# Turning the gated feed-forward tiles with transposing DMAs in two 16-bit planes instead of TensorE transposes

## The chip, the cores and the metric

The kernel runs on one core of a Trainium2 chip. The metric is the device time of one execution in microseconds (us), as the median of several runs. The profile is one execution taken by the hardware profiler. The engines are TensorE (PE for its matmuls, PEld for its weight loads), VectorE (DVE), ScalarE (ACT), GpSimd (POOL) and SyncE (SP). SP and ACT also issue DMAs from their instruction queues; in the tables these issues stand under SPq and ACTq.

## What is computed

A two-layer backbone over 256 latent tokens of width 2048, with 256 context tokens. Layer 0 mixes tokens by neighbourhood attention, layer 1 by a gated spatial MLP; each is followed by a SwiGLU feed-forward block, and every sub-layer is modulated and normalised. The change touches only the feed-forward block, which runs once in each layer, with `D_FF` = 5632:

```python
def swiglu(h, w_in, w_out):
    gate, up = jnp.split(h @ w_in, 2, axis=-1)
    return (jax.nn.silu(gate) * up) @ w_out
...
h = layer_norm(ALPHA * h + g2 * swiglu(modulate(h, sh2, sc2), ffn_w_in[i], ffn_w_out[i]), ln_g[i, 1], ln_b[i, 1])
```

All of it is float32. The kernel keeps that precision by writing each operand as a high and a low part and adding three products.

## The kernel before

**Pieces and splits.** Weights come as pieces of 128 x 1024 float32 (512 KB), loaded by SP into four `raw` buffers (L107, L108). `split_into` (L90) makes the high part with an ACT copy (L91) and the low part with a DVE subtraction (L92). During the feed-forward blocks there are five pairs of buffers for the parts, three of tag A and two of tag B (L116 to L121), so that four pieces are ready ahead of the one in use (`piece`, L125). `mm3` (L85) issues the three matmuls of a product on lines 86, 87 and 88.

**The feed-forward block.** `ffn` (L817) walks over 11 f-blocks of 512 hidden columns. For each it runs `block_T` (L792) twice: first the gate half into two PSUM accumulators `pg` (one for each 128 tokens), then the up half into `pu`. One `block_T` takes eight pieces (k2 = 0 to 7), and each piece feeds 12 matmuls: two token halves, two rows of weights, three products. After the gate half, ACT computes `sg = silu(pg)` (L843); after the up half, DVE multiplies `sg = pu * sg` (L847). That gives the gated tile in two tiles of 128 tokens x 512 columns.

**The turn.** The second projection needs the hidden columns on the partitions. So `flip` (L828) transposes each gated tile: eight TensorE transposes of 128 x 128 against an identity (L833), four into each of two PSUM tiles, and two ACT copies from PSUM to SBUF (L834). `gT` (L825) names the place: 16 hidden blocks in `gTa` and 28 in `gTb`. The two flips of an f-block are handed to the gate half of the next one as `turn`, and `block_T` pops one after its third and one after its fourth piece (L814). Those of the last f-block go into the list `side` (L849).

**The second projection.** `project_out` (L725) takes `gT` slice by slice, splits each into a high and a low part, and multiplies with the 44 pieces of the output weights, in two halves of the columns.

**Work beside it.** `tick` (L206) is called once for each piece. It pops one entry of `side`, and it pays out the modulation dot products: a list of tasks with costs, paid by a credit that grows at a fixed rate per tick (`pace`, L222) and by 0.3 of it (`BUSY`) when the tick also ran a side task. Each dot product is a 512 KB load issued by ACT (L75, into `ad`, six buffers, fetched up to five ahead) and one DVE instruction over 128 x 1024 (L150). In layer 0's feed-forward block this list is `pace(235)` (L872), in layer 1's `pace(160)` (L951).

**Order.** A scheduler orders the instructions of each engine by when they become ready, with program order as the priority. `pin` (L82) keeps an instruction behind everything that was traced before it on its engine. On each engine instructions then run strictly in that order, and an instruction that waits holds up all behind it.

Of the kernel before, what the change touches and what calls it, by code (L numbers as in the profile page):

```python
# [10 lines left out]
F32 = mybir.dt.float32  # L11
F32R = mybir.dt.float32r
BF16 = mybir.dt.bfloat16
AF = mybir.ActivationFunctionType
ALU = mybir.AluOpType
AX = mybir.AxisListType
# [2 lines left out]
P = 128  # L19
D = 2048  # L20
NT = 256
KT = D // P
NB = D // 512
# [20 lines left out]
BUSY = 0.3  # L44
# [8 lines left out]
def hybrid_kernel(ctx: ExitStack, tc: tile.TileContext, i, out):  # L53
    nc = tc.nc
    V, S, T = nc.vector, nc.scalar, nc.tensor
# [6 lines left out]
    ident = outer.tile([P, P], F32, tag="ident", name="ident")  # L62
    eps_t = outer.tile([P, 1], F32, tag="eps", name="eps_t")
    nc.gpsimd.memset(eps_t, EPS)
    warm = outer.tile([P, 1], F32, tag="warm", name="warm")
    tc.keep_in_program_order(S.activation(warm, eps_t, AF.Silu))
    lncol = outer.tile([P, 4, 2, KT], F32, tag="lncol", name="lncol")
# [14 lines left out]
    def pin(ins):  # L82
        return tc.keep_in_program_order(ins)
# [101 lines left out]
    tasks, side = [], []  # L185
    state = {"credit": 0.0, "rate": 0.0}

    def fetch_ahead():
        for t in tasks[:FETCH]:
            if t[3]:  # L190
                t[3]()
                t[3] = None
# [8 lines left out]
    def pop_task():  # L201
        fetch_ahead()
        tasks.pop(0)[2]()
        fetch_ahead()

    def tick(n=1.0):  # L206
        fetch_ahead()
        if side:
            side.pop(0)()
            n *= BUSY  # L210
        state["credit"] += n * state["rate"] if tasks else 0.0
        while tasks and state["credit"] >= tasks[0][1]:
            state["credit"] -= tasks[0][1]
            pop_task()
        if not tasks:
            state["credit"] = 0.0
# [50 lines left out]
    with tc.tile_pool(name="attnX", bufs=1) as px, ExitStack() as late:  # L267
# [21 lines left out]
        with tc.tile_pool(name="st", bufs=1) as st:  # L289
# [9 lines left out]
            held = {}  # L299
# [13 lines left out]
            pin(nc.scalar.dma_start(badj[:, 0], i["ada_b_col"][:, 0]))  # L313
            pin(S.activation(c_pad[:, :, 0:2], c_col, AF.Silu))
            pin(S.activation(c_col, c_col, AF.Silu))
            mod = st.tile([P, 2, KT, 2], F32, tag="mod", name="mod")
# [10 lines left out]
            def dot_dve(kt, t):  # L327
                r = held.pop((kt, t))
                junk = outer.tile([P, D], BF16, tag="ada", name=f"junk{kt}", bufs=ADA)
                for n, (o, bc) in enumerate(((junk, cc_bc), (r, c_bc))):  # L330
# [33 lines left out]
            def modulate(kt):  # L364
                tmp = st.tile([P, 512], F32, tag="tmp", name=f"tmp{kt}", bufs=2)
                for b in range(2):
                    sl = slice(b * 256, (b + 1) * 256)
                    S.activation(
                        tmp[:, sl], xt[kt][:, sl], AF.Identity,
                        bias=mod[:, 1, kt, b : b + 1], scale=mod[:, 0, kt, b : b + 1],  # L370
# [24 lines left out]
            for kt in range(KT):  # L395
# [35 lines left out]
                if kt == 0:  # L431
                    modulate(1)
                    for bc in (c_bc, cc_bc):
                        pin(S.activation(bc, bc, AF.Silu))
                    fetch(2)
# [4 lines left out]
                for at, h, k0 in EARLY:  # L440
                    if at == kt:
                        h += HK0
                        hi, lo = piece()
                        ps = stp_pool.tile([P, 512], F32, tag="a", name=f"eps{h}{k0}")
                        for j in range(EN):
                            c = slice(j * P, (j + 1) * P)
# [29 lines left out]
        def t_tile(name):  # L476
            return mp.tile([P, 512], F32, tag="t", name=name, bufs=2)
# [6 lines left out]
        with tc.tile_pool(name="attnB", bufs=1) as pb:  # L484
# [12 lines left out]
            def proj_q(h):  # L497
# [10 lines left out]
                ql[h] = pb.tile([P, NT], F32R, tag="ql", name=f"ql{h}", bufs=2)  # L508
                S.activation(qh[h], ps[:, 0:NT], AF.Copy, scale=SCALE)
                V.scalar_tensor_tensor(  # L510
# [133 lines left out]
    def affine_tasks(t3, src, name, rs=None):  # L644
        rows = {}

        def run(nb, b):
            def go():
                if b == 0:
                    rows[nb] = [main.tile([P, 512], F32, tag="zt", name=f"lr{name}{nb}{n}", bufs=2) for n in range(2)]  # L650
                    for n in range(2):
                        spread(rows[nb][n], src[n, nb * 512 : (nb + 1) * 512])
                sl = slice(nb * 512, (nb + 1) * 512)
                if rs:
                    normalise(t3, b, nb, rs[b])
                V.tensor_tensor(t3[:, b, sl], t3[:, b, sl], rows[nb][0], ALU.mult)
                V.tensor_tensor(t3[:, b, sl], t3[:, b, sl], rows[nb][1], ALU.add)
            return go

        side.extend(run(nb, b) for nb in range(NB) for b in range(2))  # L660

    class Modulated:
        def __init__(self, ln, layer, tsh, tsc, name):
# [125 lines left out]
                    for b in range(2):  # L789
                        finish(b, st)  # L790

    def block_T(m, ps, held, turn=()):  # L792
        xh, xl = m.xh, m.xl
        turn = list(turn)

        def products(k2, w, b):
            for kk in range(2):
                kt = k2 * 2 + kk
                c, tb = slice(kk * 512, (kk + 1) * 512), slice(b * P, (b + 1) * P)
                mm3(ps[b], xh[:, kt, tb], xl[:, kt, tb], w[0][:, c], w[1][:, c], kt == 0, kt == KT - 1)  # L800

        if held:
            ws = take(HOLD)
            for b in range(2):
                for k2 in range(HOLD):
                    products(k2, ws[k2], b)
            m.rest()
        for k2 in range(HOLD if held else 0, 8):
            with tc.issue_after(m.mark[1]) if held and k2 == HOLD else nullcontext():
                w = piece()  # L810
            for b in range(2):
                products(k2, w, b)
            tick()
            if turn and k2 >= 2:  # L814
                turn.pop(0)()

    def ffn(layer, m, key, name, finish, free, last=False):  # L817
        pg = [acc_tile(f"pg{layer}{b}") for b in range(2)]
        block_T(m, pg, True)
        free.close()  # L820
        with tc.tile_pool(name=f"ffn{layer}", bufs=1) as pf:
            g0 = outer.tile([P, KT, NT], F32, tag="xT", name=f"gTa{layer}")
            g1 = pf.tile([P, FT - KT, NT], F32, tag="gTb", name=f"gTb{layer}")

            def gT(f, n=1):  # L825
                return g0[:, f : f + n, :] if f < KT else g1[:, f - KT : f - KT + n, :]

            def flip(fb, sg, f2):  # L828
                ps = t_tile(f"gt{layer}{fb}{f2}")
                for j in range(2):  # L830
                    c = (f2 * 2 + j) * P
                    for b in range(2):
                        T.transpose(ps[:, j * NT + b * P : j * NT + (b + 1) * P], sg[b][:, c : c + P], ident)  # L833
                S.copy(gT(4 * fb + 2 * f2, 2), ps)  # L834

            turn = []
            for fb in range(FB):
                if fb:
                    pg = [acc_tile(f"pg{layer}{fb}{b}") for b in range(2)]
                    block_T(m, pg, False, turn)  # L840
                sg = [pf.tile([P, 512], F32, tag="sg", name=f"sg{layer}{fb}{b}", bufs=3) for b in range(2)]
                for b in range(2):
                    S.activation(sg[b], pg[b], AF.Silu)  # L843
                pu = [acc_tile(f"pu{layer}{fb}{b}") for b in range(2)]
                block_T(m, pu, False)
                for b in range(2):
                    V.tensor_tensor(sg[b], pu[b], sg[b], ALU.mult)  # L847
                turn = [partial(flip, fb, sg, f2) for f2 in range(2)]
            side[:0] = turn  # L849
            if last:  # L850
                last_rows()

            def extra():
                return outer.tile([P, 4, 1024], F32R, tag="xT", name=f"extra{layer}")

            project_out(FT, lambda f: gT(f)[:, 0, :], key, name, finish, extra, last)


    m = Modulated(0, 0, SH2, SC2, "f0")
# [23 lines left out]

    m = m2[0]
    affine_tasks(h_t, i["ln_row"][1], "a1")
    add_row(1, G1)
    pace(12)
# [9 lines left out]
    for nb in range(NB):  # L897
        ps = [acc_tile(f"gv{nb}{b}") for b in range(2)]
# [8 lines left out]
    def spatial(nb, g2):  # L907
        u = us[nb]
        tp = t_tile(f"uvt{nb}{g2}")
        sp = s_tile(f"sp{nb}{g2}")  # L910
        for j in range(2):
            g = nb * 4 + g2 * 2 + j
            c = slice((g2 * 2 + j) * P, (g2 * 2 + j + 1) * P)
            o = sp[:, j * NT : (j + 1) * NT].rearrange("p (b c) -> p b c", b=2)
            T.matmul(o, ws[:, g, :], vv[:, :, g * P : (g + 1) * P], start=True, stop=True)
            V.scalar_tensor_tensor(u[:, :, c], o, bs[:, g : g + 1], u[:, :, c], ALU.add, ALU.mult)
        for j in range(2):
            c = slice((g2 * 2 + j) * P, (g2 * 2 + j + 1) * P)
            for b in range(2):
                T.transpose(tp[:, j * NT + b * P : j * NT + (b + 1) * P], u[:, b, c], ident)  # L920
        S.copy(uT[:, nb * 4 + g2 * 2 : nb * 4 + g2 * 2 + 2, :], tp)

    for nb in range(NB):
        ps = [acc_tile(f"gu{nb}{b}") for b in range(2)]
# [10 lines left out]
        if nb:  # L935
            for g2 in range(2):
                spatial(nb - 1, g2)
    side.extend((lambda: spatial(NB - 1, 0), lambda: spatial(NB - 1, 1)))
    m3 = []

    def ready_f1():
# [5 lines left out]
    m = m3[0]  # L947
# [126 lines left out]
```

## Time and profile before

| | us |
|---|---|
| median of 3 runs | 2400.12 |
| lowest, highest run | 2399.07, 2402.12 |
| the profiled execution's own time | 2400.89 |
| its span, first to last instruction | 2399.1 |
| DVE busy, share of the span | 1716.8, 72% |
| ACT busy, share of the span | 1121.9, 47% |
| POOL busy, share of the span | 57.4, 2% |
| mean DMA rate | 256 GB/s |

The span is the time from the first to the last instruction; the execution's own time is 1.8 us longer. The first part of the profile gives busy times of each engine. Matmuls are pipelined and their durations overlap, so the mean duration of a matmul is longer than the time from its start to the start of the next one; a stretch's length is therefore read from start times. The second part shows the same in 40 slices of 60 us:

```profile
DVE  4877867677788778788989777686755555556666
ACT  4354434345644444444455554456444444445552
DMA  9977677766689899999989555856767666566563
```

Each digit is a busy share in tenths. The feed-forward block of layer 0 lies in slices 11 to 23, that of layer 1 in slices 28 to 40.

### The profile page before, as it was taken

Reading aid. Unit: us, or ns where it says so; the run is one execution under the profiler, and the core shown is the slowest. Engines: PE = TensorE matmul, PEld = TensorE weight load, DVE = VectorE, ACT = ScalarE, POOL = GpSimd, SP = SyncE. Lnnn points to the kernel's source line nnn. Section 1 sums busy time; section 2 is a strip of 40 time slices with the busy share of each in tenths; the row PEclk is TensorE's granted clock in tenths of the full one; section 3 lists DMA queues with packets and bytes.
Section 4 is the critical chain, followed back from the end, with each engine's and each line's share of the span. In section 5 each row is a group of like instructions: output and inputs, shape, how many; then the busy total and the mean of one; then the engine's idle time right before and its main releaser. Section 6 shows DMA issues by size and latency. Waiting matters only on the chain.

```text
span 2399.1 us, 31422 instructions
## 1 busy us (share of the span) xinstructions
PE 2370.2 (99%) x11628; PEld 1969.3 (82%) x11628; DVE 1716.8 (72%) x2297; ACT 1121.9 (47%) x1546; POOL 57.4 (2%) x63
## 2 busy tenths in 40 slices
PE   8999999999999999999999999999999999999998
PEld 6788888888788888888888788887788888888886
DVE  4877867677788778788989777686755555556666
ACT  4354434345644444444455554456444444445552
POOL 0000000000010000000000021000100000010000
PEclk9999999999999999999999999999999999999999
DMA  9977677766689899999989555856767666566563
GB/s 392 353 259 244 236 249 241 241 221 210 214 298 349 322 333 335 333 334 342 342 292 341 192 192 196 303 187 208 237 231 234 229 233 223 191 197 200 178 209 132
DMA packets 169106, 614.84 MB, mean 256 GB/s; under 512 B 19604, under 2 KB 21972, under 8 KB 164596
## 3 DMA queue, kind: packets, MB, share of 16 engines
q1 hardware_dynamic: 121172, 440.74, 53.6%
q10 hardware_dynamic: 46372, 167.86, 19.8%
q0 software_dynamic: 1408, 4.23, 0.6%
q8 instruction: 91, 1.49, 0.2%
q14 instruction: 63, 0.52, 0.1%
HBM read 610.62 MB, written 2.13 MB: 255 GB/s over the span
## 4 chain that ended last, share of the span: by engine, by line
PE 95%; DVE 2%; ACT 1%; DMA 1%; issue 1%; SPq 0%; POOL 0%; DVEq 0%; ACTq 0%; POOLq 0%
PE pu L87 7%; PE pu L88 7%; PE pu L86 7%; PE pod L86 7%; PE pod L87 6%; PE pod L88 6%; PE pg L88 6%; PE pg L86 6%; PE pg L87 6%; PE vps L86 2%; PE vps L88 2%; PE vps L87 2%; PE kps L87 2%; PE kps L88 2%; PE kps L86 2%; PE qps L86 1%
## 5 line engine op out<-in xcount | busy, mean ns | idle before, releaser
L92 DVE TENSOR_TENSOR lwf<-rwf,hwf 128x1024 fp32r<-128x1024 f32 x320 | 392.1, 1225 | 282.3 <-ACT hwf L91 281.8
L91 ACT CAST hwf<-rwf 128x1024 fp32r<-128x1024 f32 x320 | 336.2, 1051 | 483.7 <-PE pu L88 221.5
L150 DVE SCALAR_TENSOR_TENSOR ad<-ad,c_bc 128x1024 f32<-128x1024 f32 x320 | 388.0, 1219 | 0.0
L86 PE MATMUL pod<-hwd,ghd 128*128 128x512 f32 x684 | 266.5, 390 | 0.0
L87 PE MATMUL pod<-lwd,ghd 128*128 128x512 f32 x684 | 266.3, 389 | 0.0
L88 PE MATMUL pod<-hwd,gld 128*128 128x512 f32 x684 | 265.9, 389 | 0.0
L92 DVE TENSOR_TENSOR lwd<-rwd,hwd 128x1024 fp32r<-128x1024 f32 x172 | 212.1, 1234 | 63.0 <-ACT hwd L91 62.6
L91 ACT CAST hwd<-rwd 128x1024 fp32r<-128x1024 f32 x172 | 180.4, 1049 | 68.5 <-PE pod L88 45.1
L86 PEld LDWEIGHTS pod<-hwd,ghd 128*128 128x128 f32 x684 | 128.4, 188 | 27.0 <-DVE sg L847 0.3
L88 PEld LDWEIGHTS pod<-hwd,gld 128*128 128x128 f32 x684 | 128.4, 188 | 26.7
L87 PEld LDWEIGHTS pod<-lwd,ghd 128*128 128x128 f32 x684 | 128.4, 188 | 26.3
L86 PE MATMUL pg<-hwf,f0h 128*128 128x512 f32 x320 | 126.5, 395 | 0.0
L86 PE MATMUL pg<-hwf,f1h 128*128 128x512 f32 x320 | 126.5, 395 | 0.0
L88 PE MATMUL pg<-hwf,f0l 128*128 128x512 f32 x320 | 124.8, 390 | 0.0
L88 PE MATMUL pg<-hwf,f1l 128*128 128x512 f32 x320 | 124.7, 390 | 0.0
L86 PE MATMUL pu<-hwf,f1h 128*128 128x512 f32 x320 | 124.6, 389 | 0.0
L86 PE MATMUL pu<-hwf,f0h 128*128 128x512 f32 x320 | 124.6, 389 | 0.0
L88 PE MATMUL pu<-hwf,f1l 128*128 128x512 f32 x320 | 124.5, 389 | 0.0
L88 PE MATMUL pu<-hwf,f0l 128*128 128x512 f32 x320 | 124.5, 389 | 0.0
L87 PE MATMUL pu<-lwf,f1h 128*128 128x512 f32 x320 | 124.5, 389 | 0.0
L87 PE MATMUL pg<-lwf,f0h 128*128 128x512 f32 x320 | 124.5, 389 | 0.0
L87 PE MATMUL pu<-lwf,f0h 128*128 128x512 f32 x320 | 124.5, 389 | 0.0
(346 smaller groups left out, 5137.1 us busy)
## 6 DMA issues: line engine op xcount, KB each, us to landing
ad<-in_ada_t ACTq DMA_DIRECT2D x320, 512.0 KB
rwf<-in_w_in_t SPq DMA_DIRECT2D x320, 512.0 KB
rwd<-in_w_out SPq DMA_DIRECT2D x176, 512.0 KB
rwg<-in_w_gin SPq DMA_DIRECT2D x64, 512.0 KB
ap<-in_ada_p SPq DMA_DIRECT2D x20, 1024.0 KB
rwq<-in_w_q SPq DMA_DIRECT2D x32, 512.0 KB
rwo<-in_w_o SPq DMA_DIRECT2D x32, 512.0 KB
rwt<-in_w_in_t SPq DMA_DIRECT2D x32, 512.0 KB
```

What stands on the lines that cost most here:

```text
L86: keep(T.matmul(ps, sh, mh, start=first, stop=False))
L87: keep(T.matmul(ps, sh, ml, start=False, stop=False))
L88: keep(T.matmul(ps, sl, mh, start=False, stop=last))
L91: S.copy(hi, src)
L92: V.tensor_tensor(lo, src, hi.bitcast(F32), ALU.subtract)
L150: pin(V.scalar_tensor_tensor(r, r, 1.0, c_bc[:, half * 1024 : (half + 1) * 1024], ALU.mult, ALU.mult, accum_out=o[:, nt : nt + 1],))
```

## The change

A gated tile is no longer turned by TensorE. Each of its two tiles of 128 x 512 float32 is read as 128 x 512 pairs of 16-bit words. ACT copies the lower words to one plane and the upper words to another (`planes`, two copies). SP issues a transposing DMA for each plane, SBUF to SBUF, 128 x 512 words into four blocks of 128 x 128 (`turn_over`). ACT then copies the turned words of each plane to every second 16-bit place of `gT` (`join`, two copies). The tile tag `planes` has one buffer, `turned` has two, and `sg` goes from three buffers to two.

The six steps of an f-block have fixed places, counted in pieces from the end of its up half: 3, 6, 8, 11, 15 and 20. So `turn` is now a list of lists that runs on through gate halves and up halves, and the last step of an f-block comes in the gate half after the next. `side` holds lists as well, and `tick` multiplies the credit of a tick by `BUSY` once for each task.

```diff
     def tick(n=1.0):
         fetch_ahead()
         if side:
-            side.pop(0)()
-            n *= BUSY
+            for task in side.pop(0):
+                task()
+                n *= BUSY
...
-    def block_T(m, ps, held, turn=()):
+    def block_T(m, ps, held, turn=None):
         xh, xl = m.xh, m.xl
-        turn = list(turn)
...
             tick()
-            if turn and k2 >= 2:
-                turn.pop(0)()
+            if turn:
+                for task in turn.pop(0):
+                    task()
...
-            def flip(fb, sg, f2):
-                ps = t_tile(f"gt{layer}{fb}{f2}")
-                for j in range(2):
-                    c = (f2 * 2 + j) * P
-                    for b in range(2):
-                        T.transpose(ps[:, j * NT + b * P : j * NT + (b + 1) * P], sg[b][:, c : c + P], ident)
-                S.copy(gT(4 * fb + 2 * f2, 2), ps)
+            def flips(fb, sg):
+                wide = [None, None]
+                turned = [None, None]
+
+                def planes(b):
+                    wide[b] = pf.tile([P, 2, 512], U16, tag="planes", name=f"pl{layer}{fb}{b}")
+                    src = sg[b].bitcast(U16).rearrange("p (f w) -> p w f", w=2)
+                    for w in range(2):
+                        S.copy(wide[b][:, w, :], src[:, w, :])
+
+                def turn_over(b):
+                    turned[b] = pf.tile([P, 2, 4, P], U16, tag="turned", name=f"tu{layer}{fb}{b}", bufs=2)
+                    for w in range(2):
+                        pin(nc.sync.dma_start_transpose(turned[b][:, w], wide[b][:, w, :]))
+
+                def join(b):
+                    dst = gT(4 * fb, 4)[:, :, b * P : (b + 1) * P].bitcast(U16)
+                    dst = dst.rearrange("p a (t w) -> p w a t", w=2)
+                    for w in range(2):
+                        S.copy(dst[:, w], turned[b][:, w])
+
+                at = {3: (planes, 0), 6: (turn_over, 0), 8: (planes, 1), 11: (turn_over, 1), 15: (join, 0), 20: (join, 1)}
+                for n, (task, b) in at.items():
+                    while len(turn) <= n:
+                        turn.append([])
+                    turn[n].append(partial(task, b))
...
                     block_T(m, pg, False, turn)
-                sg = [pf.tile([P, 512], F32, tag="sg", name=f"sg{layer}{fb}{b}", bufs=3) for b in range(2)]
+                    block_T(m, pg, False, turn)
+                sg = [pf.tile([P, 512], F32, tag="sg", name=f"sg{layer}{fb}{b}", bufs=2) for b in range(2)]
                 for b in range(2):
                     S.activation(sg[b], pg[b], AF.Silu)
                 pu = [acc_tile(f"pu{layer}{fb}{b}") for b in range(2)]
-                block_T(m, pu, False)
+                block_T(m, pu, False, turn)
                 for b in range(2):
                     V.tensor_tensor(sg[b], pu[b], sg[b], ALU.mult)
-                turn = [partial(flip, fb, sg, f2) for f2 in range(2)]
+                flips(fb, sg)
             side[:0] = turn
```

The other entries of `side` (the affine tasks and the two last `spatial` calls) are wrapped into lists of one.

More of the change, by code (lines that the diff above doesn't have):

```diff
@@ L13 @@
 BF16 = mybir.dt.bfloat16
+U16 = mybir.dt.uint16
 AF = mybir.ActivationFunctionType
@@ L658, in run @@
             return go
-        side.extend(run(nb, b) for nb in range(NB) for b in range(2))
+        side.extend([run(nb, b)] for nb in range(NB) for b in range(2))
     class Modulated:
@@ L937, in hybrid_kernel @@
                 spatial(nb - 1, g2)
-    side.extend((lambda: spatial(NB - 1, 0), lambda: spatial(NB - 1, 1)))
+    side.extend(([partial(spatial, NB - 1, 0)], [partial(spatial, NB - 1, 1)]))
     m3 = []
```

## The prediction

> **What bounds the kernel now.** I read the busy times first, then the chain that ended last.
>
> ```profile
> PE 2370.2 (99%) x11628; PEld 1969.3 (82%) x11628; DVE 1716.8 (72%) x2297; ACT 1121.9 (47%) x1546; POOL 57.4 (2%) x63
> ...
> PE 95%; DVE 2%; ACT 1%; DMA 1%; issue 1%; SPq 0%; POOL 0%; DVEq 0%; ACTq 0%; POOLq 0%
> ```
>
> TensorE is busy for 99% of the span, and 95% of the chain is its own work. So time taken from TensorE comes off the end, as long as nothing else becomes late. The next view is the busy time by stretch, for three blocks in a row of layer 0 (gate, up, gate; each begins at the first matmul of its accumulators) and for longer stages.
>
> ```profile
> 683.60:706.35 22.75, 22.75 (x106) 18.76 (x104) 20.88 (x29) 9.39 (x10) 0.00 (x0) 1.00 0.90 316
> 706.35:728.11 21.76, 21.76 (x98) 18.02 (x96) 19.97 (x26) 11.79 (x15) 0.00 (x0) 1.00 1.01 388
> 728.11:750.86 22.75, 22.75 (x106) 18.83 (x105) 19.25 (x26) 9.99 (x11) 0.00 (x0) 1.00 0.98 361
> ...
> 683.60:1128.37 444.77, 444.77 (x2003) 368.18 (x2002) 352.69 (x444) 191.22 (x206) 2.65 (x5) 1.00 0.94 335
> 1128.37:1364.00 235.63, 235.63 (x1044) 194.86 (x1043) 204.44 (x299) 119.76 (x175) 0.00 (x0) 1.00 0.86 306
> 1702.25:2146.91 444.66, 444.66 (x2002) 368.24 (x2001) 248.04 (x253) 190.13 (x205) 2.65 (x5) 1.00 0.68 226
> ```
>
> The columns are length, then PE, PEld, DVE, ACT and POOL busy time, granted clock, DMA share and GB/s. The rows of 683.60 and 1702.25 each hold ten f-blocks (gate and up halves 2 to 11); TensorE never pauses there and its clock is full. DVE has 79% in layer 0, ACT 43%. The resource that is nearly used up beside TensorE is DMA: share 0.94 in layer 0, against 0.68 in layer 1.
>
> **What goes: the transposes.**
>
> ```profile
> L833 PE MATMUL gt<-ident,sg 128*128 128x128 f32 x176 | 26.3, 272 | 0.0
> ...
> L834 ACT COPY gTb<-gt 128x512 f32<-128x512 f32 x28 | 16.2, 579 | 3.6 <-PE gt L833 3.6
> ...
> L834 ACT COPY gTa<-gt 128x512 f32<-128x512 f32 x16 | 9.2, 579 | 0.0
> ```
>
> The mean of 272 ns is a pipelined duration, so I don't multiply by it. The stretches price the turn directly: a gate half with eight transposes takes 22.75 us, an up half with the same 96 matmuls and none takes 21.76 us. Over ten f-blocks: layer 0, 444.77 - 20 x 21.76 = 9.57 us; layer 1, 444.66 - 435.20 = 9.46 us. The eleventh turn of each layer lies in the second projection; at the same mean, 0.95 us, two make 1.9 us. **Sum: 9.57 + 9.46 + 1.9 = 20.9 us of TensorE time**, 119 ns for each of 176 transposes with what they disturb.
>
> **What comes, on ACT.** For each f-block two PSUM copies go (2 x 0.579 = 1.16 us) and eight copies of 128 x 512 16-bit words come, four `planes` and four `join`. No 16-bit copy with a stride is in the trace. The nearest row is an SBUF to SBUF copy of as many elements, the second of these:
>
> ```profile
> L91 ACT CAST hwf<-rwf 128x1024 fp32r<-128x1024 f32 x320 | 336.2, 1051 | 483.7 <-PE pu L88 221.5 <-PE pg L88 187.0 <-DMA rwf<-in_w_in_t 49.7
> ...
> L91 ACT CAST ah<-tmp 128x512 fp32r<-128x512 f32 x16 | 9.9, 620 | 0.5
> ```
>
> I take 0.62 us each; half of that is the low end (half the bytes), twice it the high one (strided words at half rate). So ACT gains 8 x 0.62 - 1.16 = 3.8 us for each f-block, on 19.1 us of 44.5 now: 22.9 of 43.5 us, 53%; 64% at the high end. What hides it are the waits of the first row: ACT mostly waits for TensorE to hand back a buffer before each cast. How late may a cast be? Three rows around one piece, ACT, ACT and DVE:
>
> ```profile
> 861.90 1.05 ACT L91 CAST hwf<-rwf 128x1024 fp32r<-128x1024 f32 x1 [1.67 <-PE pu L88]
> ...
> 864.62 1.05 ACT L91 CAST hwf<-rwf 128x1024 fp32r<-128x1024 f32 x1 [1.67 <-PE pg L88]
> ...
> 865.70 1.23 DVE L92 TENSOR_TENSOR lwf<-rwf,hwf 128x1024 fp32r<-128x1024 f32 x1 [0.35 <-ACT hwf L91]
> ```
>
> Pieces follow each other every 2.72 us; cast and subtraction are done 2.31 us after the cast starts; four pieces are ready ahead. So a cast can be 4 x 2.72 - 2.31 = 8.6 us late before TensorE waits. Two `planes` or two `join` copies, 1.24 us, fit seven times over. I cost them at nothing; without that cover they would cost 22 x 3.8 = 84 us.
>
> **What comes, on SP and DMA.** 4 transposing DMAs of 128 KB for each f-block, 88 in all. They stand in SP's queue among the raw loads:
>
> ```profile
> SPq L108 <- DVE lwf L92: 361.3, 157, 5.4
> ```
>
> In layer 0's ten f-blocks SP waited 361 of 445 us for raw buffers, 2.3 us before each load. Queued behind a transposing DMA are the next raw loads; a load that is late holds the cast, and that is the 8.6 us again. `planes` (step 3) runs on ACT beside the piece it is written at, while SP, four raw buffers ahead, comes to `turn_over` (step 6) only a piece or so later than that; so SP's wait for `planes` is about a copy long. I cost the issue at nothing.
>
> The open price is c, the time that one transposing DMA takes of all 16 DMA engines; no row shows one. Ends: by bytes, 131072 B at the highest rate of a stretch; or by runs, since a plane turns into 512 runs of 256 bytes, 32 for each engine.
>
> ```profile
> 15.00:30.00 15.00, 13.97 (x174) 10.84 (x173) 2.48 (x7) 7.81 (x10) 0.00 (x0) 1.00 1.02 412
> ...
> q1 hardware_dynamic: 121172, 440.74, 53.6%
> ...
> q10 hardware_dynamic: 290, 0.06, 3.6%
> ```
>
> Low end: 131072 B / 412 GB/s = 0.32 us. High end, each run as long as a mean packet of the weight queue: 0.536 x 16 x 2399.1 / 121172 = 0.170 us, times 32 = 5.4 us. Between them is the third row, ACT's queue in the first 8 us: 290 packets of some 210 bytes took 3.6% of 16 engines, 0.036 x 16 x 8 / 290 = 15.9 ns each. That row is nearest in size, and 32 x 15.9 ns gives **c = 0.51 us, 2.0 us for each f-block**; I take it.
>
> Does it fit in layer 0? Now an f-block moves 14.9 MB in 44.48 us. Counted by share that is 0.94 x 44.48 = 41.8 us of DMA time, by bytes at 412 GB/s only 36.2 us. After the change 43.52 us are there. With 2.0 us more: 43.8 us by share (0.3 us too much, 3 us over ten f-blocks), 38.2 us by bytes (free). The 378 to 412 GB/s in other stretches show that a share of 0.94 at 335 GB/s is partly waiting; I take the count by bytes: nothing. In layer 1 0.68 x 44.47 + 2.0 = 32.2 us, free on either count.
>
> The Trainium skill, "VectorE: DVE Perf Modes", section "The three transpose paths", speaks against this change: it lists a 128 x 128 bf16 block at 390 ns on TensorE and 1309 ns by DMA, and its rules prefer TensorE where PSUM is acceptable as the destination. By it four blocks one after another are an estimated 5.2 us for each DMA if they held all engines, and the sum would be the third rival below. No run yet shows such a DMA.
>
> **Smaller edits.** `sg` with two buffers: the second silu of the next f-block now waits for `planes` of step 8, one piece into the up half; its product is due seven pieces later (19 us), so nothing. `planes` with one buffer: step 8 waits until step 6 has landed; priced below. `tick`: after the last f-block seven tasks instead of two count `BUSY`. Layer 0 has 172 + 78 = 250 ticks; less 0.7 for each of 8 affine tasks and 7 turns 239.5, and the list is paced over 235, so the dot products still end in time; nothing.
>
> **Sum.** 2400.9 (the profiled execution's own time: span 2399.1 and 1.8 around it) - 20.9 + 0 = **2380.0 us**. That execution lies 0.8 us above the median of the runs.
>
> **Rivals.**
>
> First, layer 0 runs a little short of DMA time. For it: share 0.94. Against it: the 412 GB/s. If the share is the true demand and c = 0.67 us, then 41.8 + 4 x 0.67 = 44.5 us, the f-block of before: layer 0 gives its gain back, layer 1 keeps 9.46 + 0.95 = 10.4 us: 2390.5 us. Chance 0.17.
>
> Second, the round trip replaces the transposes as a wait. ACT stands at `planes` of step 8 until the DMAs of step 6 have landed, or at a `join`; queued behind it are the casts of the next pieces, for which TensorE waits. Two pieces lie between issue and that step, so TensorE waits when landing takes over 2 x 2.72 + 8.6 = 14.0 us, and the gain is gone at 14.0 + 0.95 = 15 us: 2400.9 us. Against it:
>
> ```profile
> 26.71 9.19 DMA ap<-in_ada_p
> ...
> gate<-gd POOLq DMA_DIRECT2D x16, 256.0 KB, 7.0
> ```
>
> The longest DMA on the chain, 1 MB in a full stage, took 9.19 us, and the broadcasts of 256 KB took 7.0 us from issue to landing (median). Chance 0.08, half of it no change, and a quarter each side.
>
> Third, slower: the DMA engines become the bound. Place: all f-blocks, layer 0 first. At the high end, c = 5.4 us, an f-block needs 41.8 + 21.6 = 63.4 us in layer 0 and 30.2 + 21.6 = 51.8 us in layer 1, where it had 44.5: 10 x (18.9 + 7.3) = 262 us, less 1.9: 2661 us. It decides from the c at which layer 0's loss eats layer 1's 10.4 us: by share 41.8 + 4c = 45.5, c = 0.93 us; by bytes 36.2 + 4c = 45.5, c = 2.3 us. For it: no row shows the operation, and the high end is far beyond both. Against it: 15.9 ns a packet puts c under both. The skill's 1309 ns a block, named above, would be this case. Chance 0.15.
>
> **How the numbers follow.** Forecast 0.60, rivals 0.17, 0.08, 0.15. A measurement of this kernel can tell about 0.2% (4.8 us) from no change. Faster: 0.60 + 0.17 + 0.02 = 0.79; same 0.04; slower 0.02 + 0.15 = 0.17. The range holds the forecast, the first rival and the second where it comes out even: from 2376 (20.9 us off the lowest run, 2399.07, gives 2378, and 2 us for the two turns that I took from a mean) to 2402. The third rival is left out.
>
> **What would show it.** Right: no L833, gate halves at 21.76 us like up halves, TensorE without idle time at L86 to L88 between 683 and 1124 us, eight ACT copies near 0.6 us for each f-block, and a DMA share in layer 0 no more than 0.05 higher. First rival: casts waiting long for `rwf`, TensorE waiting for `hwf` or `lwf` in layer 0 only. Second: ACT waiting for a DMA of `turned` or `planes` and TensorE idle behind it in both layers. Third: DMA share at 1.0 with fewer GB/s, raw loads late in both layers. The prediction is wrong if TensorE shows idle time of over 0.2 us for each f-block.

## The result and the profile after

The changed kernel takes 2465.33 us (median of 4 runs, 2458.94 to 2474.95), the kernel before 2400.74 us beside it (4 runs, 2399.07 to 2402.12): ratio 1.0273, 95% interval 1.0238 to 1.0307. The forecast was 2380 us, with a range from 2376 to 2402. The profiled execution took 2464.52 us, with a span of 2462.7.

The busy times and the chain of the work that ended last, from the changed kernel's page:

```profile
PE 2380.6 (97%) x11452; PEld 1965.5 (80%) x11452; DVE 1707.2 (69%) x2297; ACT 1194.4 (48%) x1678; POOL 55.9 (2%) x63
...
DMA packets 216978, 626.37 MB, mean 254 GB/s; under 512 B 67476, under 2 KB 69844, under 8 KB 212468
...
PE 72%; DMA 12%; DVE 8%; ACT 4%; issue 3%; SPq 1%; ACTq 0%; POOL 0%; DVEq 0%; POOLq 0%
```

The 176 transposes are gone and nothing else of TensorE's work has changed (11628 matmuls became 11452): each gate half still calls `block_T` once, so the line `+ block_T(m, pg, False, turn)` in the diff of the change is not in the kernel. Yet TensorE is busy 10 us longer than before. Its share of the chain fell from 95% to 72%, and DMA now holds 12% of it. The next view gives the busy times by stretch (columns as in the prediction): ten f-blocks of layer 0, the second projection behind them, and ten f-blocks of layer 1.

```profile
683.99:1195.50 511.51, 463.17 (x1923) 371.86 (x1922) 342.57 (x437) 222.10 (x266) 2.65 (x5) 0.95 0.99 299
1195.50:1432.00 236.50, 230.73 (x1006) 190.19 (x1005) 202.47 (x298) 121.41 (x180) 0.00 (x0) 0.99 0.89 307
1776.00:2211.80 435.80, 435.80 (x1924) 360.81 (x1923) 245.27 (x254) 224.16 (x265) 2.65 (x5) 1.00 0.86 242
```

**Layer 1 did what was forecast**: 435.8 us instead of 444.66, against 435.2 forecast, TensorE without a gap. **Layer 0 lost 67 us**: 511.5 instead of 444.8. TensorE stood idle for 511.5 - 463.2 = 48 us of it, and was busy 463.2 us for work that takes 435 us elsewhere: another 28 us. The granted clock of 0.95 explains most of these: 0.05 x 511.5 is some 26 us of full clock that were missing. The DMA share rose from 0.94 to 0.99 while the rate fell from 335 to 299 GB/s.

Three stages, between the first matmul of layer 0's ten f-blocks, that of its second projection, that of layer 1's ten f-blocks, and the end, account for 63.2 of the 63.6 us between the spans of the two profiled executions:

| | layer 0, ten f-blocks | its second projection and the mixing | from layer 1's f-blocks to the end |
|---|---|---|---|
| before | 444.8 | 573.9 | 696.9 |
| after | 511.5 | 581.0 | 686.3 |

What ended the waits in layer 0 (683.99 to 1195.5 us; total us, times, longest us):

```profile
ACT hwf L92 <- DMA rwf<-in_w_in_t: 92.2, 53, 6.2
ACT pl L838 <- DMA tu<-pl: 66.4, 7, 14.8
PEld pu L87 <- ACT hwf L92: 39.1, 13, 7.3
ACT gTa L849 <- DMA tu<-pl: 34.4, 5, 8.5
PE pu L87 <- ACT hwf L92: 33.7, 12, 6.9
ACT gTb L849 <- DMA tu<-pl: 31.3, 5, 9.9
```

Two things hold the casts that TensorE waits for. One is raw loads that are late (`hwf` waits for `rwf`, 92 us). The other is ACT standing at a `planes` or `join` copy until a transposing DMA has landed (66 + 34 + 31 = 132 us). One such place, first SP's timeline, then ACT's, then TensorE's (start, us, engine, line, what, count, idle time before it and what ended it):

```profile
940.67 3.24 SPq L843 DMA_TRANSPOSE tu<-pl  x2
```

```profile
934.63 0.62 ACT L838 COPY pl<-sg 128x512 uint16<-128x512 uint16 x1 [1.38 <-DVE sg L868]
...
941.91 1.05 ACT L92 CAST hwf<-rwf 128x1024 fp32r<-128x1024 f32 x1 [1.25 <-DVE cols L158]
...
957.80 0.62 ACT L838 COPY pl<-sg 128x512 uint16<-128x512 uint16 x1 [14.84 <-DMA tu<-pl]
```

```profile
959.42 0.80 PE L87 MATMUL pu<-hwf,f0h 128*128 128x512 f32 x1 [6.90 <-ACT hwf L92]
...
961.27 0.63 PE L89 MATMUL pu<-hwf,f0l 128*128 128x512 f32 x1
961.70 0.63 PE L87 MATMUL pu<-hwf,f0h 128*128 128x512 f32 x1
...
964.67 0.40 PE L88 MATMUL pu<-lwf,f0h 128*128 128x512 f32 x1
```

The planes of the first tile were ready at 935.7 us, but SP, which had raw loads ahead of it, came to their DMAs only at 940.7. ACT came to the planes of the second tile at 943.0. There is one `planes` buffer, so it stood 14.8 us, until the DMAs had landed 17 us after SP began to issue them, and the next cast stood behind it. TensorE lived on pieces that were ready for a while and then stood for 6.9 us; 14.8 less the 8.6 us that the prediction gave a cast is 6.2. After that gap TensorE also ran slowly for 5 us: 0.63 us instead of 0.39 for a matmul.

The copies themselves cost about what was estimated (groups of the changed kernel: count | busy, mean ns | idle before):

```profile
L92 ACT CAST hwf<-rwf 128x1024 fp32r<-128x1024 f32 x320 | 331.5, 1050 | 279.6 <-DMA rwf<-in_w_in_t 132.4
...
L838 ACT COPY pl<-sg 128x512 uint16<-128x512 uint16 x88 | 51.5, 615 | 85.2 <-DMA tu<-pl 73.1 <-DVE ad L151 6.8 <-DVE sg L868 3.6
...
L849 ACT COPY gTb<-tu 128x512 uint16<-128x512 uint16 x56 | 40.8, 767 | 59.8 <-DMA tu<-pl 58.0 <-DVE ad L151 1.9
L849 ACT COPY gTa<-tu 128x512 uint16<-128x512 uint16 x32 | 23.4, 768 | 61.7 <-DMA tu<-pl 60.6 <-DVE ad L151 1.2
```

In the prediction's row the casts mostly waited for TensorE to hand back a buffer (483.7 us of idle time, 221.5 and 187.0 of it ended by TensorE). Now the loads end the largest part, 132.4 of 279.6 us. In layer 0's ten f-blocks, by the waits above, loads end 92 us and TensorE only 5 us (3.4 and 1.9, rows further down that view): there the cover that hid the ACT work is used up.

### The profile page after: what moved, and what is told of

It reads as the page before. It is cut to its first block, busy times and chain, and to the rows that moved or that the text cites. A ratio compares the mean times of both kernels' runs of the same rounds, so it can differ in the third digit from the quotient of the medians.

```text
span 2462.7 us, 31338 instructions
## 1 busy us (share of the span) xinstructions
PE 2380.6 (97%) x11452; PEld 1965.5 (80%) x11452; DVE 1707.2 (69%) x2297; ACT 1194.4 (48%) x1678; POOL 55.9 (2%) x63
## 4 chain that ended last, share of the span: by engine, by line
PE 72%; DMA 12%; DVE 8%; ACT 4%; issue 3%; SPq 1%; ACTq 0%; POOL 0%; DVEq 0%; POOLq 0%
PE pod L89 6%; PE pod L88 6%; PE pod L87 6%; DMA tu<-pl 6%; DMA rwf<-in_w_in_t 5%; PE pu L88 3%; PE pu L89 3%; PE pu L87 3%; PE pg L89 3%; PE pg L87 3%; PE pg L88 3%; DVE lwf L93 3%; PE vps L87 2%; PE vps L88 2%; PE vps L89 2%
## 5 line engine op out<-in xcount | busy, mean ns | idle before, releaser
L92 ACT CAST hwf<-rwf 128x1024 fp32r<-128x1024 f32 x320 | 331.5, 1050 | 279.6 <-DMA rwf<-in_w_in_t 132.4
L87 PE MATMUL pu<-hwf,f0h 128*128 128x512 f32 x320 | 132.4, 414 | 33.7 <-ACT hwf L92 33.7
L88 PE MATMUL pu<-lwf,f0h 128*128 128x512 f32 x320 | 132.9, 415 | 10.0 <-DVE lwf L93 10.0
L89 PE MATMUL pu<-hwf,f0l 128*128 128x512 f32 x320 | 130.7, 408 | 0.0
```

What stands on the lines that cost most here:

```text
L87: keep(T.matmul(ps, sh, mh, start=first, stop=False))
L88: keep(T.matmul(ps, sh, ml, start=False, stop=False))
L89: keep(T.matmul(ps, sl, mh, start=False, stop=last))
L92: S.copy(hi, src)
```

## The experiments

Three theories stood for the loss in layer 0. **DMA time**: a transposing DMA takes more of the 16 DMA engines than was assumed, and layer 0 has none left. **Order**: ACT comes to `planes` and `join` before the DMA has landed, and the casts stand behind them. **SP**: each transposing DMA holds SP's queue, and with it the raw loads.

### The order pinned, and plain DMAs in place of the transposing ones

Four cells tell the first two theories apart: copies in the scheduler's order or pinned, and transposing or plain DMAs of the same bytes between the same tiles. The pinned kernels also move the steps of an f-block, so that three pieces lie between a DMA and the `planes` that waits for it (not the six or more that the expectation says). So "pinned" below always means both, the pin and the moved steps.

```diff
-                        S.copy(wide[b][:, w, :], src[:, w, :])
+                        pin(S.copy(wide[b][:, w, :], src[:, w, :]))
...
-                        S.copy(dst[:, w], turned[b][:, w])
+                        pin(S.copy(dst[:, w], turned[b][:, w]))
...
-                at = {3: (planes, 0), 6: (turn_over, 0), 8: (planes, 1), 11: (turn_over, 1), 15: (join, 0), 20: (join, 1)}
+                at = {1: (planes, 0), 4: (turn_over, 0), 7: (planes, 1), 10: (turn_over, 1), 15: (join, 0), 20: (join, 1)}
```

> The copies to planes (steps 1 and 7 instead of 3 and 8) and the joins are held at their written places in ACT's queue, so that ACT comes to each of them six or more pieces (16 us) after its DMA was issued; DMA work is the same. Theory A (layer 0 has too little DMA time): the ten f-blocks of layer 0 need at least 41.8 us by share of before and 4 x 1.7 us for the transposing DMAs (1.7 from the rise of the share in layer 1), 48.6 us each, 486 us, against 511.5 now and 444.8 before: a total of 2440 to 2465 us. Theory B (ACT stands in front of the casts, waiting for the transposes to land): the waits of pl and tu on ACT, 132 us in layer 0, go, and with them the loss: ten f-blocks in about 435 us, a total near 2385 us. Theory C (SP is held 1.28 us by each transposing DMA, so raw loads are late): as now, 2465 us.

The kernel with plain DMAs has this edit alone; its tiles are moved but not turned:

```diff
-                        pin(nc.sync.dma_start_transpose(turned[b][:, w], wide[b][:, w, :]))
+                        pin(nc.sync.dma_start(turned[b][:, w], wide[b][:, w, :].rearrange("p (a t) -> p a t", a=4)))
```

> The 88 DMAs copy the planes without transposing them, so the output is not the reference's; bytes, order and waits are the same. Theory A: a plain copy of 128 KB costs about 0.35 us of all engines by its bytes, 1.4 us for each f-block, which fits: layer 0's ten f-blocks in 435 to 440 us, a total of 2380 to 2386 us. Theory B: the round trip behind the raw loads is nearly as long, so most of the loss stays: over 2425 us. Theory C: SP is held 0.33 us instead of 1.28 us, so the loss goes: near 2382 us.

The fourth cell has both edits.

> Plain copies in place of the transposing DMAs (so the output is not the reference's) and the copies of ACT held at their written places as in e_pinned. Two causes are now supposed, each seen alone: ACT standing in front of the casts until the planes land (e_plain, where the DMA share was 0.92, still took 454.9 us for layer 0's ten f-blocks), and a shortage of DMA time from the transposition itself (e_pinned, with no wait on tu left and a share of 1.04, took 456.3 us). If these are all, this kernel has neither: layer 0's ten f-blocks in 435 to 438 us, a total near 2382 us. If a third cause is left (the eight extra ACT copies, SP's issues), it stays over 445 us.

Each ran once, and since runs of such kernels spread, all three ran again:

> The kernel of the pinned copies once more, over several runs, since single runs of these kernels spread. If two causes multiply (the order of ACT's copies and the DMA time of a transposing DMA), pinning alone leaves some 21 us of loss in layer 0's ten f-blocks and some 8 us behind them against 20.9 us of gain: 2405 to 2418 us. If the single run before was a lucky one and DMA time alone is the cause, it comes out near the changed kernel, over 2450 us.

> The kernel with plain DMAs in place of the transposing ones (its output is not turned) once more, over several runs. If two causes multiply, the order of ACT's copies alone costs some 20 us in layer 0: 2404 to 2418 us. If the transposing DMA alone is the cause, it comes out at 2380 us.

> Plain DMAs and pinned copies (the output is not turned) once more, over several runs. With both causes gone the whole gain of 20.9 us is there: 2379 to 2384 us, with a spread like that of the kernel before. A third cause would leave it above 2388 us.

The single runs took 2411.94 us (pinned), 2410.03 (plain) and 2381.03 (both). The first two lie between what the theories forecast for them, so none of the theories holds alone. With the repeats, beside 2400.72 us for the kernel before (11 runs):

| | in the scheduler's order | pinned |
|---|---|---|
| transposing DMAs | 2465.33 (the changed kernel, 4 runs) | 2420.99 (4 runs, 2415.32 to 2422.87), ratio 1.0082 (1.0068 to 1.0096) |
| plain DMAs | 2410.22 (6 runs, 2403.77 to 2415.72), ratio 1.0040 (1.0026 to 1.0054) | 2382.39 (4 runs, 2380.74 to 2384.46), ratio 0.9926 (0.9912 to 0.9939) |

With neither cause the kernel takes about what was forecast, 2382 us, and layer 0 has the forecast's length (the plain and pinned repeat, columns as before):

```profile
684.10:1119.90 435.80, 435.67 (x1922) 360.27 (x1921) 351.44 (x443) 226.97 (x264) 2.65 (x5) 1.00 0.97 353
```

The order alone costs 28 us, the transposing DMA in place of the plain one alone 39 us, the two together 83 us, which is more than their sum of 67. The pinned kernel came out 3 us above the 2405 to 2418 us that were expected of its repeat: the part of the transposing DMAs is larger than its single run had shown.

The two single causes look different in the profile. Stretches of the pinned kernel's repeat: layer 0, and the first 46 us of its second projection:

```profile
683.50:1148.70 465.20, 446.47 (x1922) 361.51 (x1921) 342.87 (x437) 221.36 (x261) 2.65 (x5) 0.99 1.04 328
1148.70:1195.00 46.30, 41.30 (x174) 33.67 (x173) 35.46 (x53) 25.44 (x38) 0.00 (x0) 0.93 1.01 317
```

And its longest waits in layer 0:

```profile
ACT hwf L92 <- DMA rwf<-in_w_in_t: 186.9, 96, 9.8
...
DVE lwf L93 <- ACT hwf L92: 119.7, 70, 8.5
```

No ACT copy waits for a transposing DMA any more; the DMA share is at 1.04 (it adds the shares of the queues, 59.2% and 43.9% for the two largest here, so it can pass 1), and the casts wait mostly for late raw loads. The backlog reaches into the second projection, which loses 5 us in its first 46.

The cells don't take the theory of SP apart from that of DMA time, since a plain DMA also holds SP for less (median 0.55 us against 1.22 in the two pinned repeats). SP had time left in the pinned repeat's layer 0: it waited 218 us for raw buffers. But it also stood 58 us until a transposing DMA and 52 us until a raw load had landed before it issued the next load, against 4.5 and 18 us with plain DMAs. The full DMA engines are the likely root of these waits, as of the late loads; how much of the 39 us comes through SP is not shown.

With plain DMAs in the scheduler's order (repeat, layer 0: stretch, then waits) it is the other way round (the execution shown, 2403.77 us, is the fastest of the six):

```profile
683.80:1131.80 448.00, 441.52 (x1923) 363.21 (x1921) 340.62 (x433) 222.80 (x265) 2.65 (x5) 0.99 0.93 339
```

```profile
ACT hwf L92 <- DMA rwf<-in_w_in_t: 93.5, 66, 4.3
ACT pl L838 <- DMA tu<-pl: 35.1, 7, 7.1
ACT gTb L849 <- DMA tu<-pl: 21.5, 8, 5.4
ACT gTa L849 <- DMA tu<-pl: 19.7, 5, 6.3
```

The share is 0.93, no more than before the change, and ACT stands 76 us at `planes` and `join`.

### Layer 0 without its modulation loads

The 176 loads of 512 KB for the modulation products in this stage, and 16 more of the mixing stage behind it, are left out (192 of 320 in all), and with them ACT's time to issue them; DVE does the same instructions on a tile that is resident. The transposing DMAs and the scheduler's order stay.

```diff
+            if key[:2] == (0, G2) or (layer == 1 and t != G2):
+                loaded[key] = None
+                return
...
-                r, r, 1.0, c_bc[:, half * 1024 : (half + 1) * 1024], ALU.mult, ALU.mult,
+                r, got, 1.0, c_bc[:, half * 1024 : (half + 1) * 1024], ALU.mult, ALU.mult,
```

> The loads of 176 modulation weights in layer 0's feed-forward stage are left out (VectorE reads a resident tile in their place, with the same instructions), so the output is not the reference's. Theory A: demand in layer 0 falls by 6.3 MB for each f-block, about 17 us, to 48.6 - 17 = 32 us, under the 43.5 us of TensorE: ten f-blocks in 435 us, a total near 2385 us. Theory B: landing becomes as quick as in layer 1, where ACT still waited 52 us for it, so a part of the loss may go as well; at least 30 us of ACT waiting on tu or pl stays in layer 0. Theory C: SP is held as long as before, the loss of 67 us stays: 2465 us.

2380.64 us (one run). Layer 0's stretch, then its waits (`join` is line 856 there):

```profile
684.50:1119.80 435.30, 435.30 (x1922) 360.54 (x1921) 342.98 (x436) 223.97 (x265) 2.65 (x5) 1.00 0.76 210
```

```profile
ACT gTa L856 <- DMA tu<-pl: 32.9, 8, 6.1
ACT gTb L856 <- DMA tu<-pl: 20.8, 12, 3.1
```

The whole loss is gone at a DMA share of 0.76, though SP is held by as many transposing DMAs and ACT still stands 54 us at `join`. So with spare DMA time SP's hold costs nothing, and waits of up to 6 us are covered by the 8.6 us of a cast. In these runs either cause reached TensorE only where the DMA engines had little spare time: at a share of 0.93 and more in layer 0, not at 0.76 here nor at 0.86 in layer 1.

### The price of one transposing DMA

The kernel before, with 16 transposing DMAs of the same shape and then 16 plain ones, all on SP, behind its last block.

```diff
+        for n in range(16):
+            s = src[:, (n % 8) * 512 : (n % 8 + 1) * 512]
+            pin(nc.sync.dma_start_transpose(tz[:, n], s))
...
+        for n in range(16):
+            s = src[:, (n % 8) * 512 : (n % 8 + 1) * 512]
+            pin(nc.sync.dma_start(cz[:, n], s.rearrange("p (a t) -> p a t", a=4)))
```

> The kernel before, and at its end, with nothing beside them, 16 transposing DMAs of 128 x 512 words in a row, a wait, and 16 plain copies of the same planes; the output is unchanged. If the price of a transposing DMA is that of its 256-byte runs at 15.9 ns a packet, 16 take 8 to 10 us (0.51 us each) unless SP's issue is slower. If it is what the share in layers 0 and 1 rose by (1.2 to 1.8 us), 16 take 20 to 29 us. SP was held 1.28 us by each in the changed kernel; held so here, 20.5 us. The plain copies: 0.35 us each by bytes or 0.33 us by SP's issue, 5 to 7 us for 16.

One run, 2412.61 us; the DMAs ran just ahead of the last output stores.

The instructions of the two targets (min/median/max ns, first and last start):

```profile
L978 SPq DMA_TRANSPOSE tz<-c_bc x16: 1239/1266/2015, 2369.5 to 2390.0; - x16
...
L983 SPq DMA_DIRECT2D cz<-c_bc x16: 465/599/609, 2393.1 to 2404.9; - x16
```

The DMA queue from 2371 to 2391 us (packets, MB, share of 16 engines), while only transposing DMAs run:

```profile
q1 hardware_dynamic: 8061, 1.94, 60.6%
```

SP is held 1.27 us by each, and they follow each other at that distance: SP's issue, not the engines, is the limit here. The engines were busy 0.606 x 20 = 12.1 us for 1.94 MB, which is 14.8 DMAs of 131072 B: **0.82 us of all 16 engines each**, or 0.606 x 20 x 16 / 8061 = 24.1 ns for a 256-byte packet. The same sum over 4.3 us of the plain DMAs (0.67 MB at a share of 47.1%) gives 0.40 us; a plain one held SP for 0.60 us, not the 0.33 us expected. Under load the price of a transposing DMA seems higher, in estimates from the shares: in layer 0 the pinned repeat's DMAs cost (1.04 x 465.2 - 0.94 x 444.8) / 40 = 1.6 us each, and in layer 1 the changed kernel's cost (0.86 x 435.8 - 0.68 x 444.7) / 40 = 1.8 us. They are rough: the pinned copies in layer 1 below give (0.80 x 435.2 - 0.68 x 444.7) / 40 = 1.1 us, and the plain, pinned kernel in layer 0 gives (0.97 x 435.8 - 0.94 x 444.8) / 40 = 0.1 us for a DMA that took 0.40 us alone, so a part of the share before the change was waiting, as the prediction said. And at the 1.7 us of the expectation above, an f-block of the pinned kernel would have taken 48.6 us; it took 45.6 and 46.5.

### Only layer 1, and layer 0 in part

TensorE turns layer 0's tiles as before the change; layer 1 keeps the transposing DMAs.

```diff
             def flips(fb, sg):
+                if layer == 0:
+                    turn.extend([[], [], [partial(flip, fb, sg, 0)], [partial(flip, fb, sg, 1)]])
+                    return
```

> Layer 0 turns its tiles on TensorE as before, layer 1 by transposing DMAs. All theories expect layer 1 to keep its gain: ten f-blocks 435.3 us instead of 444.7 and 0.95 us for the eleventh, 10.3 us: 2390.4 us, a ratio of 0.9957. If layer 1 only gained because layer 0 was late (its loads or dot products shifted), the gain is smaller.

2391.82 us (5 runs, 2389.27 to 2393.40), ratio 0.9958 (0.9944 to 0.9971). Its layer 1 has 435.7 us for ten f-blocks, its layer 0 the 444.7 of before. The same with the pinned copies in layer 1:

> TensorE turns layer 0's tiles as before, transposing DMAs turn those of layer 1, and there the copies are pinned at their written places. If the unpinned version of this lost its last 2 us in the eleventh turn of layer 1 or in the order of ACT's copies, this gains them back: 2389 to 2390 us. If the order of the copies costs nothing where DMA time is left over, it stays at 2391.8 us.

2390.87 us (5 runs, 2389.63 to 2392.62), ratio 0.9961 (0.9947 to 0.9975). Layer 0, then layer 1:

```profile
684.90:1129.80 444.90, 444.90 (x2002) 368.16 (x2001) 352.21 (x444) 191.29 (x206) 2.65 (x5) 1.00 0.94 335
1704.00:2139.20 435.20, 435.20 (x1922) 360.37 (x1921) 247.94 (x253) 225.39 (x263) 2.65 (x5) 1.00 0.80 241
```

The median is 1 us lower, less than these intervals can tell: where DMA time is left over the order costs little. Both versions beat the kernel before, by 9.6 and 9.9 us of the 10.4 that layer 1 was forecast to bring, and the changed one.

Two tries to save layer 0's half failed. In the first, one of the two tiles of each f-block in layer 0 is turned by TensorE, the other by DMA, pinned:

```diff
+                if layer == 0:
+                    at = {2: (flip, 0), 3: (planes, 1), 6: (turn_over, 1), 14: (join, 1)}
```

> Layer 1 turned by transposing DMAs, in layer 0 one of the two tiles of an f-block by TensorE and the other by DMA, copies of ACT held at their written places. Half of the transposing DMAs in layer 0: the share of e_pinned, 1.04 x 45.6 = 47.4 us for each f-block, falls by half of the 5.6 us that it stood over the 41.8 of before: 44.6 us, at 1.04 in 42.9 us, below TensorE's 44.0. So layer 0 gains 0.48 us for each f-block and layer 1 10.4 us: 2385.8 us, ratio 0.9935. If any transposing DMA in layer 0 costs more than it saves: above the 2391.8 us of e_layer1.

2401.06 us (12 runs, 2388.43 to 2415.11), ratio 1.0002 (0.9984 to 1.0020). The profiled execution (2393.67 us), layer 0 and then its second projection:

```profile
683.90:1124.60 440.70, 440.53 (x1963) 364.21 (x1962) 349.05 (x440) 209.82 (x236) 2.65 (x5) 1.00 1.02 343
1124.60:1360.00 235.40, 231.43 (x1008) 190.32 (x1007) 200.87 (x295) 119.22 (x175) 0.00 (x0) 0.99 0.88 301
```

Layer 0 gained 4 us of the 4.8 forecast, at a share of 1.02, and the next stage lost 4 us of TensorE time. This execution is 7 us below the median; what the slower ones lose beyond that is not shown. In the second, all tiles are turned by DMA, pinned, and the loads of 32 dot products move from layer 0 to the mixing stage behind it:

```diff
-    add_dots(1, SH1, SC1, G1, SC2)
+    add_dots(1, SH1, SC1, G1)
...
+    add_dots(1, SC2)
+    pace(50)
```

> All tiles turned by transposing DMAs, copies of ACT held at their written places, and 32 of the 176 modulation dot products with their loads moved from layer 0's feed-forward stage into the gated MLP stage after it, where the DMA share was 0.56 to 0.86. If DMA time is the only cause left in e_pinned, layer 0's demand falls by 1.1 MB for each f-block, about 3 us of 47, and nearly fits: ten f-blocks in 435 to 445 us, a total of 2381 to 2392 us. If the residue of e_pinned is something else, 2410 us as there.

2397.55 us (12 runs, 2389.56 to 2407.96), ratio 0.9995 (0.9980 to 1.0009). Layer 0, and 80 us of the mixing stage:

```profile
684.10:1119.50 435.40, 435.40 (x1923) 360.38 (x1923) 323.82 (x399) 223.94 (x264) 2.65 (x5) 1.00 1.03 327
1480.00:1520.00 40.00, 36.47 (x154) 29.65 (x154) 33.43 (x47) 15.89 (x20) 3.29 (x2) 0.91 0.81 279
1520.00:1560.00 40.00, 38.23 (x174) 31.04 (x173) 33.97 (x50) 15.97 (x18) 0.00 (x0) 1.00 0.94 341
```

Layer 0 took 435.4 us, as forecast, in this execution, but the moved loads made the mixing stage late: TensorE lost 5 us in these two stretches, where the kernel before has 40.00 us of it in both. This execution (2389.56 us) is the fastest of the twelve, 8 us below the median, so it shows a part of what is lost and not all of it.

## Why the prediction was wrong

**What held.** The sum of 20.9 us for the transposes: layer 1 alone brings 9.6 to 9.9 us of it, and with plain DMAs and pinned copies the kernel takes 2382 us, 18 us below the kernel before; the other 2 to 3 us were not looked for. The ACT copies: 0.615 and 0.767 us against 0.62. The structure of a transposing DMA: the packets rose by 47872 and the traffic by 11.53 MB, which is 88 times 512 + 32 packets and 131072 B. The 8.6 us that a cast may be late: a stand of 14.8 us came through as 6.9 us, so 7.9 us were hidden.

**The step that failed first** is "32 x 15.9 ns gives c = 0.51 us, ... I take it", and with it "I take the count by bytes: nothing". Measured, a packet takes 24.1 ns with nothing beside it and one DMA gives each of the 16 engines 34 of them (512 runs and 32 small packets), so c = 0.82 us. In the full layer 0 it was more, an estimated 1.0 to 1.6 us: (45.6 - 41.8) / 4 = 0.95 from the shorter f-block below, and the 1.6 by share above. The row of 15.9 ns was the nearest in size, but of another kind of DMA, from the first 8 us of the kernel. The count was the worse half: with 0.82 us, four DMAs would have fitted by bytes (36.2 + 3.3 = 39.5 of 43.5 us for each f-block), but not by share (41.8 + 3.3 = 45.1). With the pinned copies, where no landing holds ACT any more, the f-block took 45.6 us in the first run's profile and 46.5 in the second's: the count by share was near, and a little mild still. It also lets the plain DMAs fit (41.8 + 4 x 0.40 = 43.4), as they did. The 1.0 to 1.6 us are worked out from the length of these same f-blocks, so they are no second proof of it. This is the place of the third rival, whose price by share was c = 0.93 us, though in layer 0 only.

**The second failure** is the place of ACT and SP. The prediction let "two pieces lie between issue and that step" and let SP come to `turn_over` "only a piece or so later". In the trace SP came to the DMAs 5 us after their planes, with raw loads ahead of it, and ACT made one cast between the issue and the copy that waits. So TensorE is hit when the landing comes some 11 us after SP's issue (943.0 - 940.7 = 2.3 us until ACT stands there, and 8.6), not 14.0. The landing itself was misjudged too: it came 17 us after the issue, past the 14.0 as well, where the prediction had taken 9.19 and 7.0 us from other DMAs as its ground for a chance of 0.08. And the prediction counted the same 8.6 us as cover for ACT's copies, for late raw loads and for late landings, each by itself; in layer 0 the casts met all three. The `join` copies weren't at their written places either. The first one of layer 0 is written nine pieces behind its DMA; ACT's timeline has it two casts behind the DMA's issue at 698.6 us:

```profile
699.42 1.06 ACT L92 CAST hwf<-rwf 128x1024 fp32r<-128x1024 f32 x1 [0.81 <-DMA rwf<-in_w_in_t]
...
700.66 1.05 ACT L92 CAST hwf<-rwf 128x1024 fp32r<-128x1024 f32 x1 [0.18 <-DMA rwf<-in_w_in_t]
...
710.02 0.77 ACT L849 COPY gTa<-tu 128x512 uint16<-128x512 uint16 x1 [8.31 <-DMA tu<-pl]
```

`join` isn't pinned, and the scheduler moved it ahead. That the order of ACT's copies is a cause, and not only beside it, the plain kernels show: with the order pinned 28 us go, and no copy of ACT waits for a landing any more. Whether the pin or the moved steps of those kernels did more wasn't tried.

**Why the two multiply.** Full DMA engines make the transposing DMAs land late, 15.4 us for one on the chain; late landings hold ACT; and ACT also issues the modulation loads, so these stop as well (two were issued at once at 710.02 us, when the `join` above was released). That the order costs 28 us with plain DMAs and 44 us (2465.33 - 2420.99) with transposing ones is measured; this chain between them is read from the timelines and was not tried by itself.

**The rivals.** The first (2390.5 us, layer 0 gives its gain back) was too mild, the second had the right place on ACT but called for both layers, and the third had the right engine but was set aside because of the 15.9 ns row. The Trainium skill, "VectorE: DVE Perf Modes", section "The three transpose paths", has 1309 ns for a 128 x 128 block by DMA. The four blocks of one DMA took 1.27 us of SP's time and 0.82 us of the engines here, so the prediction's estimate of 5.2 us from that figure isn't borne out. The preference for TensorE, in the section "Rules for kernel authors" of the same page of the Trainium skill, is borne out in layer 0 and not in layer 1.

**The chances.** 0.79 for faster rested on the count by bytes. Two counts that disagree by 5.6 us for each f-block, with 0.3 us over by the stricter one, were no ground for 0.60 on the milder.

## What to carry to other kernels

Where a stage has a DMA share of 0.94, count a new transfer by share, not by bytes at the best rate seen elsewhere (the count by share can be too strict, but here it put both the plain and the transposing DMAs on the right side), and try it in the stage that has DMA time left before all stages. A transfer that takes the place of a short engine operation brings a consumer that stands in an engine's queue: look where the scheduler puts that consumer, and pin it behind the landing as it is under load. Small transposing DMAs should be priced by a run of their own, since no row of the profile before showed their packet time or how long they hold the queue that issues them.

## What the hardware showed that was not expected

- A transposing DMA of 128 KB holds SP for 1.27 us, a plain one of the same bytes for 0.60 us.
- A gap of TensorE costs more than its length. After the 6.9 us gap above, matmuls took 0.63 us for 5 us (granted clock 0.74 from 952 to 965 us), and in layer 0 of the changed kernel such stretches make most of the 28 us that came on top of 48 us of idle time. The Trainium skill, "TensorE: Matmul & The Clock Gate", section "Part 1: The HAM clock gate (the "warmup" mystery)", puts the array at half its clock after an idle window of about 3.4 us. The rate agrees, start to start 0.43 us instead of 0.23; the length of the gap does not always: in the same trace matmuls also went to 0.63 us after gaps of 1.52 and 0.76 us with one matmul between them (778.97 and 780.23 us; granted clock 0.66 from 779 to 784 us).
- Nearer to full DMA engines (layer 0's share 1.02 against 0.94) the time was less steady: 12 runs of the kernel with half of layer 0's tiles spread over 27 us, the 23 of the kernel before beside them over 8 us.
